# A rewritten first stage with unsplit modulation weights, a new panel order, and eight seven-product gate panels

## The chip, the cores and the metric

The kernel runs on one core of one Trainium2 chip. The metric is the device time of one execution in microseconds (us). Engines: PE (TensorE, matrix products; its weight loads are listed apart as PEld), DVE (VectorE), ACT (ScalarE), POOL (GpSimd), and SP, whose queue issues most transfers.

## The reference

One layer of a decoder trunk runs for a prompt group (1024 tokens) and a sample group (8 sequences of 8 tokens), 1088 tokens in all, with shared weights. The model width is 1024.

- `mod = silu(c) @ w_mod + b_mod` gives shift, scale and gate (each 1024 wide) for nine condition vectors: one of the prompt, eight of the samples.
- `h = rmsnorm(x, norm_g) * (1 + scale) + shift`, and `proj = h @ w_in`, whose columns are three merge gates (mg, 3 x 1024), u, va, za (spatial gating), q, k, v, ob, zb (mLSTM with four heads), p, zc (causal pooling) and eight gate columns.
- Three branches turn these into ya, yb and yc; each is projected (`w_br_a`, `w_br_b`, `w_br_c`), weighted by `sigmoid(mg)`, summed, projected by `w_out`, multiplied by `gate`, added to x and normalised.
- The states of the mLSTM and of the pooling, and the normalised va rows of the samples, are returned too.

All in float32. The kernel keeps the accuracy by splitting a float32 operand into a rounded high part and a low rest (`split`, line 206: a cast on ACT, a subtraction on DVE) and adding three products: high x high, high x low, low x high.

## The kernel before

All instructions of an engine run in the order in which the program issues them; waits between engines are semaphores. Large tiles come from one pool of 34 `slots` (128 x 1088 float32); PSUM has eight banks.

**Weights.** `Stream` (line 37) loads weight panels (1024 x 256) in quarters over SP's queue, and `step` (line 103) splits one quarter: cast on ACT (line 132), subtraction on DVE (line 101). `prep_some` and `seven` call it between matmuls.

**Panels.** `b_panel` (line 258) makes transposed output: six units (two halves of 128 columns by three token groups of 364, 362, 362), each with 8 x 3 matmuls; with `kouter` all six units are open at once and are evicted at the end. `a_panel` (line 296) makes token-major output, nine units of 24 matmuls with 256 columns (16 for the sample unit). `seven` (line 334) makes a panel with seven block products in place of eight: 7 x 2 x 4 x 3 matmuls of 272 columns, the sums of blocks being made on DVE.

**Side work.** Generators in `self.side` are advanced by `tick` between half units; `self.pace` says how many steps a unit gives. Their matmuls stand in PE's list among those of the panels. `drain` runs what is left.

**Order.** `start` (line 466); panels q2 and q3; 25 seven-product panels (k, zb, zc, u, za and five of the twelve mg panels, `MG7 = 5`); p0, va0, p1, va1, ... ; v0 to v3; ob0 to ob3; mg panels 5 to 11; the branch projections in the order c, a, b (four panels each, `finish`, line 1718); the output projection. Gates, spatial gating (`gen_sgu`), gate row (`gen_gate`, line 867), samples (`gen_sample`) and prompt mLSTM (`gen_prompt`) are side work from v0 on.

**The first stage.** A string of letters, `PLAN_0 + PLAN_1` (line 1853), is run letter by letter, and each calls a small function. `1` loads a panel of `w_mod`, `2` an x tile (128 features x 1088 tokens), `3` a weight quarter. `S` splits half a modulation panel, `M` multiplies it (line 548), `C` and `T` copy and turn the result into columns `am` (scale) or `sm` (shift). `Q` squares an x tile on ACT and adds it up on POOL (line 581). `A` or `V` scale x by `am`, `H` and `L` split it. `W` splits a weight quarter; `P` and `R` multiply one x tile with panel q0, later q1: 12 and 6 matmuls (line 614). `e` sums the squares over features with ones as the second operand (line 625), `f` spreads the norm over partitions (line 641). `v` (DVE) or `g` (POOL, line 648) multiply x by the norm, `m` adds the shift and splits the result into the tiles `h` (lines 653 to 660). `z`, `s`, `t` multiply the shift columns with q0 and q1; `r` evicts raw rows. The rows of q0 and q1 get the norm on POOL (line 705) and the shift in `finish_rows`. `gen_factors` (line 757) adds high and low parts again and forms the block sums for `seven`; `put_t4` overwrites part of h with the last of them, after its last use in q3.

Of the kernel before, what the change touches and what calls it, by code (L numbers as in the profile page):

```python
# [32 lines left out]
MG7 = 5  # L33
PACE = 1.5
# [124 lines left out]
class Builder:  # L159
# [98 lines left out]
    def b_panel(self, panel, acts, evac, nk=KT, kouter=False, hook=None):  # L258
# [3 lines left out]
        units = [(f, g) for f in range(2) for g in range(3)]  # L262
# [22 lines left out]
        for u, (f, g) in enumerate(units):  # L285
# [7 lines left out]
            self.tick(self.pace / 2)  # L293
        self.st.used(panel)
# [119 lines left out]
    def body(self):  # L414
# [7 lines left out]
        for nm_, ns in [(x, (n,)) for n in range(4) for x in ("p", "va")] + [(x, range(4)) for x in ("v", "ob")]:  # L422
# [43 lines left out]
    def start(self):  # L466
# [10 lines left out]
        raws, wsp, pmod, xs, xsp = {}, {}, {}, {}, {}  # L477
        panels = (4, 5, 6, 7, 0, 1, 2, 3)

        def mod_load():  # L480
            n = nxt("ml")
            raws[n] = [self.slot([128, 4, 256], name="ss") for _ in range(2)]
            m = 4 if n else 2
            for j in range(0, KT, m):
                S.dma_start(raws[n][j // 4][:, j % 4 : j % 4 + m], i["w_mod"][panels[n]][:, j : j + m, :])
# [6 lines left out]
        cT = self.slot([128, KT, 9], name="cT")  # L492
        S.dma_start(cT, i["cT"])
        mod_load()
        sel = self.cload("sel")
# [17 lines left out]
        self.scs = self.slot([128, KT, 64], F32R, name="scs")  # L513
        V.tensor_copy(self.scs, zero.unsqueeze(1).to_broadcast([128, KT, 64]))
        sc = self.const([128, KT, 9], "sc")
# [3 lines left out]
        A.copy(self.scs[:, :, 0:9], sc)  # L519
        V.tensor_tensor(out=self.scs[:, :, 32:41], in0=sc, in1=self.scs[:, :, 0:9].bitcast(F32), op=ALU.subtract)  # L520
# [9 lines left out]
        def mod_split():  # L530
            n, j = divmod(nxt("ms"), 2)
            raw = raws[n][j]
            hi = self.slot([128, 4, 256], F32R, name="ssh")
            lo = self.slot([128, 4, 256], F32R, name="ssl")
            m = 4 if n else 2
            for q in range(0, 4, m):
                self.split(*(x[:, q : q + m] for x in (raw, hi, lo)))
            wsp.setdefault(n, []).append((hi, lo))
            if j:
                raws.pop(n)  # L540

        def mod_mul():
            n = nxt("mm")
            p = pmod[n] = self.ps()
            w = wsp.pop(n)
            for kk in range(KT):
                for j in range(2):
# [195 lines left out]
        def hook(k):  # L743
            for j in range(2):
                if k == j + 1:
                    self.put_t4(j)
# [1218 lines left out]
```

## Time and profile before

| | us |
|---|---|
| median of 3 runs (1856.19 to 1857.31) | 1856.73 |
| the profiled execution | 1857.86 |
| its span, first to last instruction | 1856.1 |
| busy: PE, DVE, ACT, POOL | 1796.1, 1071.9, 586.0, 262.3 |
| first stage, to the first matmul of q2 | 119.3 |
| to the first matmul of the seven-product panels | 176.9 |
| end of the seven-product panels | 707.3 |

The granted clock of PE has a mean of 0.985; in the profile's strip of 40 slices it is below full in three of the first four slices. A matmul's entry lists the moving operand first, then the stationary one with its rows and columns (`128*128`), then the moving shape. A float32 matmul whose operands aren't split shows as two records.

### The profile page before, as it was taken

To read this page: it belongs to the slowest core of one execution; us is meant where nothing else is said; L and a number is where in the kernel's file an instruction comes from. 1 tells how busy PE (TensorE), PEld (TensorE's weight loads), DVE (VectorE), ACT (ScalarE), POOL (GpSimd) and SP (SyncE) were. 2 spreads that over 40 slices of the span, in tenths; PEclk is the share of its full clock that TensorE was granted. 3 is DMA by queue.
4 is the path that set the end of the run, shared out by engine and by line. 5 is a ranking of instruction groups with operands and counts; after the bars stand their busy time and mean duration, and the time that the engine had idled before them with its cause. 6 is when DMAs were issued, how large, how long until landed. Compare 5 with 4: busy or idle time off the path is not lost.

```text
span 1856.1 us, 32242 instructions
## 1 busy us (share of the span) xinstructions
PE 1796.1 (97%) x13017; PEld 1777.4 (96%) x13017; DVE 1071.9 (58%) x2003; ACT 586.0 (32%) x1141; POOL 262.3 (14%) x427
## 2 busy tenths in 40 slices
PE   7888999999999999999999999999999999999998
PEld 7888999999999998999999899999999999999998
DVE  7777556665666542434527955664655766564444
ACT  5443333333333332222223125332333231131224
POOL 3440000000000001110011212321101101200023
PEclk8988999999999999999999999999999999999999
DMA  6332323332222334333335754776457577694422
GB/s 252 108 128 74 106 94 94 104 122 80 71 70 76 130 106 150 121 123 101 94 116 189 217 180 125 240 237 201 143 175 231 179 228 208 184 317 142 151 62 97
DMA packets 142152, 270.42 MB, mean 146 GB/s; under 512 B 19377, under 2 KB 66161, under 8 KB 142003
## 3 DMA queue, kind: packets, MB, share of 16 engines
q1 hardware_dynamic: 118786, 184.20, 31.4%
q0 software_dynamic: 23072, 83.91, 13.3%
q8 instruction: 102, 1.67, 0.4%
q14 instruction: 48, 0.39, 0.1%
q10 hardware_dynamic: 144, 0.26, 0.0%
HBM read 179.96 MB, written 88.35 MB: 145 GB/s over the span
## 4 chain that ended last, share of the span: by engine, by line
PE 86%; DVE 8%; issue 2%; DMA 2%; ACT 1%; POOL 1%; SPq 0%; POOLq 0%; DVEq 0%; ACTq 0%
PE ps L270 30%; PE ps L308 15%; PE p L362 8%; PE y L362 8%; PE z L362 8%; PE x L362 4%; PE ps L614 2%; PE ps L316 1%; PE ps L1466 1%; PE ps L1264 1%; PE ps L1485 1%; PE ps L1682 1%; PE ps L1439 1%; PE ps L1468 1%; DMA ss<-in_w_mod_dram 1%
## 5 line engine op out<-in xcount | busy, mean ns | idle before, releaser
L101 DVE TENSOR_TENSOR wlo<-raw,whi 128x512 fp32r<-128x512 f32 (+1 forms) x272 | 189.7, 698 | 115.6 <-ACT whi L132 115.6
L308 PE MATMUL ps<-whi,hhi 128*128 128x256 f32 (+1 forms) x768 | 218.5, 284 | 0.0
L308 PE MATMUL ps<-wlo,hhi 128*128 128x256 f32 (+1 forms) x768 | 216.0, 281 | 0.0
L308 PE MATMUL ps<-whi,hlo 128*128 128x256 f32 (+1 forms) x768 | 215.1, 280 | 0.0
L270 PE MATMUL ps<-hhi,whi 128*128 128x362 f32 (+1 forms) x624 | 208.2, 334 | 5.5 <-DVE C L1494 3.4
L270 PE MATMUL ps<-hlo,whi 128*128 128x362 f32 (+1 forms) x624 | 207.0, 332 | 1.9 <-DMA hlo<-b12d 1.7
L270 PE MATMUL ps<-hhi,wlo 128*128 128x362 f32 (+1 forms) x624 | 206.6, 331 | 0.0
L270 PE MATMUL ps<-yhi,whi 128*128 128x362 f32 (+1 forms) x576 | 190.1, 330 | 3.0 <-DVE mgr L1742 1.6
L270 PE MATMUL ps<-yhi,wlo 128*128 128x362 f32 (+1 forms) x576 | 188.7, 328 | 0.0
L270 PE MATMUL ps<-ylo,whi 128*128 128x362 f32 (+1 forms) x576 | 188.5, 327 | 0.0
L132 ACT CAST whi<-raw 128x512 fp32r<-128x512 f32 (+1 forms) x272 | 162.3, 617 | 44.9 <-DVE raw L123 36.3
L308 PEld LDWEIGHTS ps<-whi,hhi 128*128 128x128 f32 x768 | 144.6, 188 | 0.8 <-issue 0.4
L308 PEld LDWEIGHTS ps<-wlo,hhi 128*128 128x128 f32 x768 | 144.7, 188 | 0.0
L308 PEld LDWEIGHTS ps<-whi,hlo 128*128 128x128 f32 x768 | 144.4, 188 | 0.0
L270 PEld LDWEIGHTS ps<-hhi,whi 128*128 128x128 f32 x624 | 119.2, 191 | 6.7 <-DVE C L1494 3.6
L362 PE MATMUL p<-hhi,whi 128*128 128x272 f32 x400 | 116.1, 290 | 7.3 <-ACT row L859 7.3
L270 PEld LDWEIGHTS ps<-hlo,whi 128*128 128x128 f32 x624 | 119.5, 191 | 2.6 <-DMA hlo<-b12d 2.6
L270 PEld LDWEIGHTS ps<-hhi,wlo 128*128 128x128 f32 x624 | 119.4, 191 | 0.0
L362 PE MATMUL p<-hlo,whi 128*128 128x272 f32 x400 | 116.5, 291 | 0.0
L362 PE MATMUL p<-hhi,wlo 128*128 128x272 f32 x400 | 116.3, 291 | 0.0
L132 ACT CAST whi<-sum 128x512 fp32r<-128x512 f32 x75 | 46.6, 621 | 219.7 <-DVE sum L119 144.0
L270 PEld LDWEIGHTS ps<-yhi,whi 128*128 128x128 f32 x576 | 108.2, 188 | 3.7 <-DVE mgr L1742 1.8
(434 smaller groups left out, 4489.6 us busy)
## 6 DMA issues: line engine op xcount, KB each, us to landing
raw<-in_w_in_dram SPq DMA_DIRECT2D x204, 256.0 KB
mgr<-mgd SPq DMA_DIRECT2D x24, 544.0 KB
raw<-in_w_br_dram SPq DMA_DIRECT2D x48, 256.0 KB
out_dram<-C POOLq DMA_DIRECT2D x36, 256.0 KB, 4.5
ylo<-yd SPq DMA_DIRECT2D x16, 544.0 KB
merd<-mgr POOLq DMA_DIRECT2D x16, 544.0 KB, 6.1
C<-in_state_C_dram SPq DMA_DIRECT2D x32, 256.0 KB
mgd<-mg POOLq DMA_DIRECT2D x14, 544.0 KB, 4.6
```

Source lines behind the costliest of these rows:

```text
L101: self.kb.V.tensor_tensor(out=lo, in0=src, in1=hi.bitcast(F32), op=ALU.subtract)
L132: kb.A.copy(hi, src)
L270: self.PE.matmul(ps[:, :n], part(panel, w, k, fs), a[:, g0 : g0 + n], start=(k == 0 and j == 0), stop=(k == nk - 1 and j == 2))
L308: self.PE.matmul(p[:, :cols], a[:, ts], part(panel, w, k, cs), start=(k == 0 and j == 0), stop=(k == KT - 1 and j == 2))
L316: self.PE.matmul(p[:, :cols], stack[:, k, :], part(panel, j, k, cs), start=(k == 0 and j == 0), stop=(k == KT - 1 and j == 1))
L362: PE.matmul(bank[n][:, g, :HT], w[:, ks], b[:, gs], start=(n in (1, 5, 6, 7) and j == 0 and m == 0), stop=(j == 3 and m == 2), skip_group_ ...
L614: PE.matmul(sums[-1][u][:, :m], self.st.part(w, 1 - ww, k, fs), a[:, g0 : g0 + m], start=(k == 0 and part == "high" and j == 0), stop=(k = ...
L1264: self.PE.matmul(p[:, :n], wsl[:, ww, k, fs], a[:, g0 : g0 + n], start=(k == 0 and j == 0), stop=(k == 1 and j == 2))
L1439: PE.matmul(x["ps"][:, h * 128 : h * 128 + 128], k[:, 2 * h + d, :], q[:, 2 * h + d, :], start=(d == 0), stop=(d == 1))
L1466: PE.matmul(p[:, :258], x["qw"][:, 2 * h + d, :], C[x["hp"]][:, h, d, :], start=(d == 0), stop=False)
L1468: PE.matmul(p[:, :258], x["P"][:, a, h, :], x["vs"][:, b, h, :], start=(x["c"] == 0 and j == 0), stop=(j == 2))
L1485: PE.matmul(p[:, :258], x["ks"][:, a, h, d * 128 : d * 128 + 128], x["vs"][:, b, h, :], start=(j == 0), stop=(j == 2))
```

## The change

- **Modulation.** `S`, `C`, `T` are gone. `mod` multiplies the unsplit float32 weights, 128 x 128 at a time as the stationary operand, by the nine columns `sc`, and its result is already turned. The same holds for `gen_gate`, whose result is turned back by eight transposes.
- **Squares.** Each squared tile is summed over its features on PE at once (`square_sum`, letter `U`, nine matmuls with one column) into one bank, in place of the additions on POOL.
- **x and h.** `H` scales and casts in one ACT instruction and `L` scales and subtracts in one DVE instruction, so x stays unscaled; `v` scales by `am` and the norm in one; `m` adds the shift to x in place and splits it. x is kept in float32, and `gen_factors` takes it from there. No tile-wide work is left on POOL in this stage.
- **Plans.** New strings for `PLAN_0` and `PLAN_1`; loads stand two groups ahead.
- **q2, q3.** All four `gen_factors` are side work from q2 on; q3 runs unit by unit with token groups in the order 2, 1, 0, and `put_t4` follows units four and five. `b_panel` gets `order` and calls `hook` after each unit.
- **Order.** p0, v0, p1, v1, ...; then va0 to va3, ob0 to ob3. Side work: gates, samples, spatial gating, sample output (`gen_sample_out`, split off), prompt. `gen_gate` moves under the last branch projection. `MG7` is 8, `PACE` 1.4 throughout.

```diff
-MG7 = 5
-PACE = 1.5
+MG7 = 8
+PACE = 1.4
...
+        units = [divmod(u, 3) for u in order]
...
+            if hook is not None:
+                hook(u)
...
-        for nm_, ns in [(x, (n,)) for n in range(4) for x in ("p", "va")] + [(x, range(4)) for x in ("v", "ob")]:
+        for nm_, ns in [(x, (n,)) for n in range(4) for x in ("p", "v")] + [(x, range(4)) for x in ("va", "ob")]:
...
+        def mod():
+
             n = nxt("mm")
...
+            raw = raws.pop(n)
             p = self.ps()
...
             for j in range(2):
...
+                v = p[:, j * 16 : j * 16 + 9]
+                for kk in range(KT):
+                    PE.matmul(v, raw[kk // 4][:, kk % 4, j * 128 : j * 128 + 128], sc[:, kk, :], start=(kk == 0),
+                              stop=(kk == KT - 1))
...
+        def square_sum():
+            k = nxt("us")
+            sq = sqs.pop(k)
             if k == 0:
...
+                acc.append(self.ps())
+            for t in range(9):
+                m = 128 if t < 8 else 64
+                PE.matmul(acc[0][:m, t : t + 1], sq[:, t * 128 : t * 128 + m], ones, start=(k == 0 and t == 0),
+                          stop=(k == KT - 1), skip_group_check=True)
...
+        def h_scale():
+            k = nxt("hs")
+            x = xs[k]
+            V.scalar_tensor_tensor(out=x[:, :TP], in0=x[:, :TP], scalar=am[:, k, 0:1], in1=rb[0][:, :TP], op0=ALU.mult,
+                                   op1=ALU.mult)
+            V.tensor_tensor(out=x[:, smp], in0=x[:, smp], in1=rb[0][:, smp], op=ALU.mult)
+            V.tensor_tensor(out=bview(x[:, smp]), in0=bview(x[:, smp]), in1=bcol(sm[:, k, 1:9]), op=ALU.add)
...
+            A.activation(x[:, :TP], x[:, :TP], AF.Identity, bias=sm[:, k, 0:1])
+            self.split(x, hh, hl)
...
+        while len(self.side) > 2:
+            self.advance(self.side)
+
+        def hook(u):
+            if u == 2:
+                self.drain()
+            if u > 3:
+                for j in range(2):
+                    self.put_t4(2 * u - 8 + j)
+
+        self.b_panel(self.pan["q", 3], self.h, self.evac_rows(3, self.qd), hook=hook, order=(2, 1, 0, 5, 4, 3))
...
+                for k in range(KT):
+                    PE.matmul(p[:, j * 16 : j * 16 + 9], w[k // 4][:, k % 4, j * 128 : j * 128 + 128], self.sc[:, k, :],
+                              start=(k == 0), stop=(k == KT - 1))
...
+        self.side += [self.gen_gates(), self.gen_sample(), self.gen_sgu(), self.gen_sample_out(), self.gen_prompt()]
...
+                if n == 0 and xi == 2:
+                    self.side.append(self.gen_gate())
...
 Builder.PLAN_0 = (
-    "wSS3w21M2W2CT1QVwSH4SL2wPQMV2Q1CWTHR21VSPHLSPMQ3Q2RVHLRLCTPVWSRHL23SPWQQMC3RVTHAHLLwPRQV3H"
-    "LPSSRPR1WS3"
+    "1223w 1223QQwMHHWLLw 1223UUQQMPHHWPLLRR 1223UUQQMPHHWPLLRR 13UUQQMPHHWPLLRR 13UUWPPRRe"
 )
 Builder.PLAN_1 = (
-    "rW13SeSM1CPP3MS3PCfRTSgMCgPWSvRgTMgCRTvRTPzmWRmsmgPmPWmWgPRRmtms3R3WmW3tr"
+    "r13WMfPR fW13MPRvm PRvmWPRvmM 33PRvm33PRvmMzs PRvmWWPRvmsWW vmr"
 )
```

More of the change, by code (lines that the diff above doesn't have):

```diff
@@ L482, in mod_load @@
             raws[n] = [self.slot([128, 4, 256], name="ss") for _ in range(2)]
-            m = 4 if n else 2
-            for j in range(0, KT, m):
-                S.dma_start(raws[n][j // 4][:, j % 4 : j % 4 + m], i["w_mod"][panels[n]][:, j : j + m, :])
+            for j in range(2):
+                S.dma_start(raws[n][j], i["w_mod"][panels[n]][:, 4 * j : 4 * j + 4, :])
         def x_load():
@@ L528, in start @@
         self.h = []
[L530 to L542, printed above, removed]
-            n = nxt("mm")
[L544 to L547, printed above, removed]
-                    PE.matmul(p[:64, :256], self.scs[:, kk, :], w[kk // 4][j][:, kk % 4, :],
-                              start=(kk == 0 and j == 0), stop=(kk == KT - 1 and j == 1))
-        def mod_copy():
-            n = nxt("mc")
-            t = self.tmp.tile([64, PW], F32, tag="smp", name=self.nm("smp"), bufs=2)
-            A.copy(t[:, :256], pmod[n][:64, :256])
-            pmod[n] = t
-        def mod_turn():
-            n = nxt("mt")
-            t = pmod.pop(n)
+        def mod():
+            n = nxt("mm")
+            raw = raws.pop(n)
             p = self.ps()
-            if n == 0:
-                V.tensor_scalar(bmod[:, 1, :], bmod[:, 1, :], 1.0, None, ALU.add)
             for j in range(2):
-                PE.matmul(p[:, j * 16 : j * 16 + 9], t[:, j * 128 : j * 128 + 128], sel, start=True, stop=True)
+                v = p[:, j * 16 : j * 16 + 9]
+                for kk in range(KT):
+                    PE.matmul(v, raw[kk // 4][:, kk % 4, j * 128 : j * 128 + 128], sc[:, kk, :], start=(kk == 0),
+                              stop=(kk == KT - 1))
             for j in range(2):
@@ L617, in mms, with rms @@
                 xsp[k] = None
-            if n == KT - 1 and part == "low":
-                self.st.units -= 4
-        def rms_sum():
-            p = self.ps()
-            for t in range(9):
-                m = 128 if t < 8 else 64
-                PE.matmul(p[:m, t : t + 1], acc[0][:, t * 128 : t * 128 + m], ones, start=True, stop=True)
+        def rms():
+            p = acc.pop()
             ms = self.const([128, 9], "ms")
@@ L631, in rms_sum @@
             self.rsqrt(rs, ms, rt)
[L632 removed]
+            rb.append(self.slot([128, T], name="rb"))
         def rms_rows():
[L635 to L644 removed]
@@ L646, in h_scale @@
-        def h_scale(eng):
-            x = xs[nxt("hs")]
-            eng.tensor_tensor(out=x, in0=x, in1=rb[0], op=ALU.mult)
+            b = nxt("rr")
+            t0, t1 = ((0, 4), (4, 9))[b]
+            ps = [self.ps() for _ in range(-(-(t1 - t0) // 4))]
+            for t in range(t0, t1):
+                m = 128 if t < 8 else 64
+                o = (t - t0) % 4 * 128
+                PE.matmul(ps[(t - t0) // 4][:, o : o + m], rs[:m, t : t + 1].to_broadcast([m, 128]), self.ident[:m, :m],
+                          start=True, stop=True)
```

212 lines of the change are left out of this document (84 added, 128 removed).

## The prediction

> **What bounds the kernel now.** I read the page first, then busy time by stage, then the chain of waits and the order of PE's work in the first 180 us.
>
> ```profile
> span 1856.1 us, 32242 instructions
> PE 1796.1 (97%) x13017; PEld 1777.4 (96%) x13017; DVE 1071.9 (58%) x2003; ACT 586.0 (32%) x1141; POOL 262.3 (14%) x427
> ```
>
> PE is the bound: what lengthens its list lengthens the kernel, unless it lands in idle time of PE. Nearly all of that lies early, as the table by stage shows (columns: stretch, its length, busy time of PE, PEld, DVE, ACT and POOL with instructions, granted clock, DMA share, GB/s):
>
> ```profile
> 0.00:119.30 119.30, 95.05 (x604) 89.30 (x604) 92.28 (x108) 57.36 (x81) 49.87 (x31) 0.89 0.47 166
> 119.30:143.00 23.70, 23.70 (x130) 23.69 (x130) 14.62 (x23) 11.81 (x20) 7.79 (x7) 0.89 0.50 173
> 143.00:176.80 33.80, 26.59 (x161) 26.30 (x159) 30.01 (x37) 12.96 (x23) 1.06 (x2) 0.93 0.08 26
> 176.80:707.30 530.50, 530.43 (x4200) 530.22 (x4200) 305.46 (x461) 179.64 (x303) 21.81 (x42) 0.99 0.30 96
> ```
>
> The rows are the first stage, panel q2, panel q3 and the 25 seven-product panels. Only the first and third have slack. The chain says why:
>
> ```profile
> 106.25 7.89 DVE x L653
> 119.38 22.41 PE ps L270 x120
> 174.64 2.18 ACT row L859 x6
> 176.87 5.78 PE p L362 x24
> 182.64 3.02 PE y L362 x24
> 1201.36 3.99 PE ps L270 x24
> ```
>
> ```profile
> 116.00 0.21 DVE L653 TENSOR_TENSOR x<-x,sm 128x64 f32<-128x64 f32 x1
> 109.13 4.92 POOL L705 TENSOR_TENSOR row<-row,rb 128x1088 f32<-128x1088 f32 x2
> ```
>
> An addition over 64 columns that elsewhere takes 0.21 us held VectorE for 7.9 us while POOL multiplied rows of the same stage (the change moves that work off POOL); q3 with its six banks open ended in six evictions, with PE idle for 7.3 us; and the first seven product then took 5.78 us against 3.02 for a later one.
>
> **Part 1, dense prices.** Full-clock matmuls cost 3.99/24 = 0.166 us in a b-panel and 3.02/24 = 0.126 in a seven-product panel. A b-panel has 144 (23.9 us), a seven panel 168 (21.2). Three panels changed: 3 x 2.7 = **-8.1 us**. Their VectorE work lies under PE: 305 us busy of 530 in that stage, 12 a panel; without that cover it would cost up to 3 x 12 us.
>
> **Part 2, tiny matmuls.** The new `mod` multiplies 128x128 weights by nine columns: 16 matmuls a panel; `square_sum` has nine with one column for each x tile. The nearest rows:
>
> ```profile
> 60.16 2.04 PE L625 MATMUL ps<-ones,acc 128*128 128x1 f32 x18
> 71.79 2.31 PE L641 MATMUL ps<-c_ident,rs 128*128 128x128 f32 x18
> 37.19 1.02 PE L564 MATMUL ps<-c_sel,smp 64*128 64x9 f32 x4
> 48.10 0.61 PE L564 MATMUL ps<-c_sel,smp 64*128 64x9 f32 x4
> 8.87 0.28 PE L548 MATMUL ps<-ssl,scs 128*64 128x256 f32 x1
> 28.58 0.28 PE L548 MATMUL ps<-ssh,scs 128*64 128x256 f32 x1
> 28.70 0.28 PE L548 MATMUL ps<-ssl,scs 128*64 128x256 f32 x1
> L897 PE MATMUL ps<-wgs,scs 128*64 128x256 f32 x64 | 7.9, 276 | 0.0
> ```
>
> Nine matmuls are 18 records at 0.112 us, so two a matmul. `mod` is then 32 x 0.112 = 3.6 us and one x tile's sum 2.0. Removed are 16 x 0.115 (starts 28.58 to 28.70) = 1.8 and a turn of 0.6. Over eight of each, PE's list grows by 8 x 1.2 + 7 x 2.0 = 24 us, more than the 119.3 - 95.1 = 24 us that PE idles. `gen_gate`, now under the last branch, goes from 64 x 0.115 = 7.4 us to 128 x 0.112 plus eight transposes at 0.11 = 15.2: **+7.8 us**, since PE is dense there.
>
> [...]
>
> **Part 3, the clock, which decides.** At 37.19 the same four records cost 1.02 us, not 0.61: the clock was at half. It changes in steps of 3.41 us. Stretches cut at those steps (PEclk is the third number from the end):
>
> ```profile
> 86.90:90.31 3.41, 1.90 (x12) 1.65 (x12) 2.71 (x6) 0.00 (x0) 0.04 (x1) 1.00 0.00 0
> 90.31:93.72 3.41, 3.41 (x13) 3.38 (x14) 1.96 (x7) 1.93 (x5) 0.17 (x1) 0.50 0.00 0
> 711.54:714.95 3.41, 1.94 (x12) 1.56 (x10) 0.00 (x0) 0.24 (x1) 0.47 (x2) 1.00 1.03 418
> 714.95:718.36 3.41, 1.75 (x7) 0.75 (x5) 0.00 (x0) 0.49 (x2) 0.30 (x2) 1.00 1.03 397
> 1080.18:1083.59 3.41, 2.04 (x17) 1.81 (x16) 3.38 (x6) 0.38 (x1) 0.58 (x1) 1.00 0.64 243
> 1083.59:1087.00 3.41, 3.41 (x17) 3.18 (x16) 1.15 (x1) 0.00 (x0) 1.67 (x2) 0.50 0.73 163
> 1493.19:1496.60 3.41, 1.85 (x13) 1.64 (x12) 2.03 (x5) 0.00 (x0) 0.00 (x0) 1.00 0.73 224
> 1496.60:1500.01 3.41, 3.41 (x26) 3.41 (x25) 3.24 (x14) 0.47 (x1) 1.51 (x2) 1.00 0.05 11
> ```
>
> Busy time doesn't order them: after 1.90 and 2.04 us the clock fell, after 1.94 and 1.85 it stayed. What does is that the first two held narrow matmuls:
>
> ```profile
> 88.41 0.61 PE L564 MATMUL ps<-c_sel,smp 64*128 64x9 f32 x4 [1.78 <-DVE sm L571]
> 88.95 1.26 PE L614 MATMUL ps<-xlo,whi 128*128 128x364 f32 x6
> 1082.38 1.07 PE L1029 MATMUL ps<-c_w_sguS,va 64*128 64x64 f32 x8 [1.36 <-ACT tok L971]
> 40.72 0.50 PE L614 MATMUL ps<-xhi,whi 128*128 128x362 f32 x1
> 41.02 0.51 PE L614 MATMUL ps<-xhi,wlo 128*128 128x362 f32 x1
> ```
>
> Between 86.90 and 90.31 only six wide matmuls (6 x 0.166 = 1.0 us, 29%) count, if nine-column ones do not. I take it that streamed columns keep the clock up and records do not. In the new stage `UUM` is 68 tiny records, 7.6 us without a wide matmul, over two steps long, ahead of `PPRR`, 36 wide ones in 6.0 us. At half clock a wide one costs 0.30 (40.72 to 41.02) and, in that ratio, a tiny one 0.2; the clock returns after one wholly wide step, as at 1083.59.
>
> **Part 4, the first stage summed.** From when the first weights are in (about 7 us; the old first panel's last product starts at 8.87): `M U U M` is 100 records, the clock falls near 8.4: 12 x 0.112 + 88 x 0.2 = 19, to 26. `PPRR` then has half clock until one whole step has passed, on average 1.5 steps = 5.1 us (17 matmuls), the other 19 at 0.166: 8.3, to 34.3. Two further groups: on average 5.1 us at full clock (46 records), 22 x 0.2 = 4.4, then 8.3: 17.8 each, to 69.9. `UU PPRR`: 4.0 + 8.3, to 82. The second part is four `M` (14.3), eight `PR` (8 x 18 x 0.166 = 23.9), the broadcasts of the norm (2.3, as at 71.79) and two shift products (2 x 1.84): 44; a lone `M` of 3.6 us, scarcely one step, loses about 2, so +8: PE reaches q2 at 134.
>
> Beside it runs a chain on VectorE and ScalarE, in which `v m` works one x tile at a time, each step waiting for the other engine:
>
> ```profile
> L658 DVE SCALAR_TENSOR_TENSOR hlo<-x,sm,hhi 128x1024 fp32r<-128x1024 f32 x8 | 10.2, 1278 | 4.4 <-ACT hhi L656 4.3
> L656 ACT ACTIVATE hhi<-x,sm 128x1024 fp32r<-128x1024 f32 x8 | 9.2, 1147 | 0.0
> L595 ACT CAST xhi<-x 128x1088 fp32r<-128x1088 f32 x8 | 8.8, 1098 | 12.8 <-DVE x L590 12.8
> L208 DVE TENSOR_TENSOR t<-fac,t 128x1088 fp32r<-128x1088 f32 x4 | 5.1, 1284 | 1.1 <-ACT t L207 1.1
> ```
>
> 1.28 + 1.15 + 1.10 + 1.28 and hops make 5.0 us a tile, 40 for eight, 44 with five weight splits and the shift. It starts when the norm's rows are out (82 + 12 = 94) and ends at 138, when q2's first unit asks for the last tile (134 + 3.5). I add 4 us for what meets there: a bank for the sixth `M`; the shift product, which waits for its split with the last two `PR` queued behind it on PE; the last tile, for which the whole of q2 waits. Bounds: 0 and twice that. What gets late next is q2, which ends at 138 + 4 + 20.5 = 162.5. The turn of the shift (0.9), q3 now unit by unit (23.9) and one eviction (0.7) bring the first seven product to **188**, against 176.87: +11.1. Its product then runs at full clock: 3.02 - 5.78 = -2.8. At nothing I cost `gen_factors` and `finish_rows` (about 32 us of VectorE under q2 and q3, 48 us) and the new order of v, va and the samples, whose matmuls and loads are the same. The first stage's loads come in groups on SP's queue, two groups ahead of PE, with nothing else on it; the gate's eight loads now stand on that queue among those of the last branch. The bounds for these are in the rivals.
>
> Sum against the profiled execution's 1857.9: +11.1 - 2.8 - 8.1 + 7.8 = +8.0, so 1865.9; the median shown is 1.1 below it: **1865 us**.
>
> **The rivals.** *The clock holds (faster).* If weight loads count as activity, PE has no idle step and all is at 0.112 and 0.166: `PPRR` of the first group ends at 7 + 11.2 + 6 = 24.2, two groups of 13.6 and one of 10 bring 61.4, the norm's rows are out at 71, the chain ends at 115, q2 at 135.5, and with 3 us for the idle PE before it the seven products start at 164: -12.9 - 2.8 - 0.3 = -16, **1841**. For it: no narrow stretch of over 2.3 us is in the trace. Against it: with narrow ones counted in full, 1.90 us should have held the clock as 1.85 and 1.94 did. It decides if the granted clock is 1.00 through a `UUM`.
>
> [...]
>
> *Only the long stretches fall.* A lone `M` costs nothing and the chain of 44 sets q2: the four us added and 2 of the chain's start go, 182: **1859**.
>
> *A late stall (slower).* The samples now run before the gating unit, whose two constant tiles are then still held, among 34 slots. If each of their 32 steps waits 0.3 us for a load, 10 us come on top: **1875**. The same price covers a merge load that waits behind the gate's on SP. Against it, the longest wait of these products in the old run:
>
> ```profile
> PE ps L1682 <- DVE Cs L208: 0.5, 1, 0.5
> ```
>
> *The seven panels give nothing*, if VectorE can't keep up: +8.1, **1873**; 58% busy there speaks against it.
>
> **How the numbers follow.** Forecast 0.47, only long stretches 0.12, late stall 0.08, seven panels nothing 0.04, clock holds 0.29. The range is 1839 to 1876; the likeliest's own is 1858 to 1873. A measurement of this kernel can tell about 0.2%, 3.7 us: faster 0.29, same 0.13 (the second rival and the forecast's lower end), slower 0.58.
>
> **What will show it.** Granted clock near 0.5 to 0.8 in slices one to three with PE busy throughout; tiny records at 0.2 us; the first seven product near 188 us and at 3.0; the gate's records at 0.112 under the last branch. The forecast is wrong if the clock stays at 1.00 there, or if q2 starts before 125 us.

## The result and the profile after

The changed kernel takes **1898.25 us** (median of 4 runs, 1895.33 to 1901.06) against 1857.02 for the kernel before (4 runs, 1856.19 to 1858.02): a ratio of 1.0222, 95% interval 1.0204 to 1.0239. It is 41 us slower, 33 us over the forecast of 1865 and outside its range. The profiled execution took 1898.14 us.

The head of the page of the changed kernel, busy time and the 40 slices:

```profile
span 1896.0 us, 32907 instructions
PE 1847.7 (97%) x13367; PEld 1830.7 (97%) x13367; DVE 1033.1 (54%) x2016; ACT 585.5 (31%) x1123; POOL 213.3 (11%) x410
...
POOL 0000000000000000010101223322101101200023
PEclk6789999999999999999999999999999999999999
```

PE is as busy as before (97%), with 350 instructions more. What stands out is the granted clock, well below full in the first three slices, 142 us. The same by stage (columns: stretch, its length, busy time of PE, PEld, DVE, ACT and POOL with instructions, granted clock, DMA share, GB/s); the first row is the kernel before up to its first seven product, the others are the changed kernel:

```profile
0.00:176.90 176.90, 145.37 (x893) 139.32 (x893) 136.92 (x167) 82.15 (x122) 58.73 (x40) 0.90 0.40 140
```

```profile
0.00:198.30 198.30, 192.37 (x1099) 190.10 (x1099) 82.34 (x149) 68.97 (x98) 10.57 (x23) 0.79 0.36 129
...
198.00:789.00 591.00, 590.74 (x4703) 590.74 (x4704) 338.69 (x511) 202.61 (x341) 25.57 (x48) 1.00 0.30 96
789.00:1896.00 1107.00, 1064.61 (x7568) 1049.89 (x7567) 612.08 (x1357) 314.20 (x686) 177.14 (x339) 0.98 0.52 170
```

Three differences make up the 40.3 us between the two profiled executions:

- **First stage: +21.4 us.** The first seven product starts at 198.3 instead of 176.9. PE now idles only 6 us there (198.3 - 192.4) where it idled 31.5, but its clock averages 0.79 instead of 0.90. Length times clock is 159 us of full-clock time before and 157 after, which suggests, without showing it, that with the clock of before the stage would be no longer than it was.
- **Seven panels: as forecast.** 28 in 591.1 us, 21.1 each; 25 took 530.4.
- **Late part: 21.7 us over the forecast's account.** From the last seven product (789.4) to the end it is 1106.6 us, against 1148.8 from 707.3 on before. Three panels of 23.9 us less and 7.8 of gate more would have given 1084.9. (21.4 + 60.7 - 42.2 = 39.9, the difference of the spans.)

The waits of TensorE behind the first stage (columns: the matmul that waited and for whom; total us, times, longest):

```profile
PE ps L1637 <- DVE qz L1601: 13.3, 3, 6.8
PE ps L986 <- DVE va L976: 8.0, 5, 4.0
PE ps L270 <- DMA hlo<-b12d: 2.6, 2, 1.7
PE ps L1637 <- ACT Cs L207: 2.3, 2, 1.3
PE ps L1637 <- DVE Cs L208: 2.3, 4, 1.2
```

L1637 is the sample product, L1682 in the kernel before, where it waited 0.7 us in all. Now it waits 17.9, most of it at three points, where the samples pass from one head to the next (L1601). Summed over the gaps between all matmuls behind the last seven product, PE idles 32.4 us against 18.6 before. The rest of the 21.7, some 8 us, is records that take longer: 36.7 us of this part go by at half clock, against 14.7 before. The falls stand at 797.8 (10.2 us, where the first panel behind the sevens waits for its transfers `hlo<-b12d`; 3.4 us at the same place before), at the two longest waits of the samples (6.8 us at 1122.1, 10.2 at 1180.1) and at the longest of the gating unit (L986, 3.4 us at 1221.0); the rest is at the very end. The matmuls behind the first of the samples' two cost 0.21 us each, where 12 of them in a dense panel take 1.38 us, 0.115 each:

```profile
1122.98 1.20 PE L1637 MATMUL ps<-Cs,qz 128*128 128x258 f32 x4 [4.93 <-DVE qz L1601]
...
1124.62 0.42 PE L310 MATMUL ps<-wlo,hhi 128*128 128x256 f32 x1
1124.83 0.42 PE L310 MATMUL ps<-whi,hlo 128*128 128x256 f32 x1
```

### The profile page after: what moved, and what is told of

The parts are those of the page before. It is cut to its first block, busy times and chain, and to the rows that moved or that the text cites. A ratio compares the mean times of both kernels' runs of the same rounds, so it can differ in the third digit from the quotient of the medians.

```text
span 1896.0 us, 32907 instructions
## 1 busy us (share of the span) xinstructions
PE 1847.7 (97%) x13367; PEld 1830.7 (97%) x13367; DVE 1033.1 (54%) x2016; ACT 585.5 (31%) x1123; POOL 213.3 (11%) x410
## 5 line engine op out<-in xcount | busy, mean ns | idle before, releaser
L270 PE MATMUL ps<-yhi,whi 128*128 128x362 f32 (+1 forms) x576 | 190.9, 331 | 0.6 <-DVE vo L1463 0.6
L270 PE MATMUL ps<-yhi,wlo 128*128 128x362 f32 (+1 forms) x576 | 188.6, 327 | 0.0
L270 PE MATMUL ps<-ylo,whi 128*128 128x362 f32 (+1 forms) x576 | 188.4, 327 | 0.0
L270 PE MATMUL ps<-hhi,whi 128*128 128x362 f32 (+1 forms) x480 | 161.2, 336 | 3.5 <-ACT hhi L207 1.8
L270 PE MATMUL ps<-hlo,whi 128*128 128x362 f32 (+1 forms) x480 | 160.6, 335 | 3.6 <-DMA hlo<-b12d 2.6
L270 PE MATMUL ps<-hhi,wlo 128*128 128x362 f32 (+1 forms) x480 | 159.8, 333 | 0.0
L364 PE MATMUL p<-hhi,whi 128*128 128x272 f32 x448 | 128.7, 287 | 0.6 <-ACT row L824 0.6
L364 PE MATMUL p<-hlo,whi 128*128 128x272 f32 x448 | 129.1, 288 | 0.0
L364 PE MATMUL p<-hhi,wlo 128*128 128x272 f32 x448 | 128.9, 288 | 0.0
L132 ACT CAST whi<-sum 128x512 fp32r<-128x512 f32 x84 | 52.1, 620 | 245.5 <-DVE sum L119 165.6
L270 PEld LDWEIGHTS ps<-yhi,whi 128*128 128x128 f32 x576 | 108.4, 188 | 0.9 <-DVE vo L1463 0.9
L270 PEld LDWEIGHTS ps<-ylo,whi 128*128 128x128 f32 x576 | 108.4, 188 | 0.1
L270 PEld LDWEIGHTS ps<-yhi,wlo 128*128 128x128 f32 x576 | 108.4, 188 | 0.0
L270 PEld LDWEIGHTS ps<-hlo,whi 128*128 128x128 f32 x480 | 92.4, 192 | 5.2 <-DMA hlo<-b12d 4.0
```

The source lines that it names most:

```text
L132: kb.A.copy(hi, src)
L270: self.PE.matmul(ps[:, :n], part(panel, w, k, fs), a[:, g0 : g0 + n], start=(k == 0 and j == 0), stop=(k == nk - 1 and j == 2))
L364: PE.matmul(bank[n][:, g, :HT], w[:, ks], b[:, gs], start=(n in (1, 5, 6, 7) and j == 0 and m == 0), stop=(j == 3 and m == 2), skip_group_ ...
```

## The experiments

Two questions: is it the clock that makes the first stage long, and what makes the samples wait? My theory for the first is the forecast's part 3 (narrow matmuls do not hold the clock); the rival is that the narrow records cost what they cost. For the second I began with late state loads, against a burst of VectorE work, the new order, and lack of room beside the shorter late part.

| kernel | what differs | us, median | ratio to before, 95% |
|---|---|---|---|
| changed | | 1898.3 | 1.0204 to 1.0239 |
| e_mix | narrow and wide matmuls 1 : 1 | 1925.0 | 1.0326 to 1.0385 |
| e_fill | a zero matmul behind each narrow one | 1981.0 | 1.0647 to 1.0680 |
| e_rows | modulation streams the weights | 1903.6 | 1.0236 to 1.0285 |
| e_pool | and squares summed on GpSimd | 1883.3 | 1.0123 to 1.0171 |
| e_chain | and first stage reordered | 1877.8 | 1.0106 to 1.0139 |
| e_order | later panels in the old order | 1900.4 | 1.0216 to 1.0251 |
| e_order5 | and five mg panels as sevens | 1887.6 | 1.0149 to 1.0179 |
| e_load | state loads one pair earlier | 1893.5 | 1.0172 to 1.0216 |
| e_head | masked keys made step by step | 1918.5 | 1.0315 to 1.0345 |
| e_slots | two constant tiles loaded late | 1883.3 | 1.0128 to 1.0162 |
| e_slotload | e_slots and e_load | 1877.3 | 1.0101 to 1.0131 |
| e_best2 | e_chain and e_slotload | 1858.0 | 0.9996 to 1.0032 |
| e_best3 | and two waits removed | 1863.9 | 1.0022 to 1.0050 |
| e_best4 | and the gate from split weights | 1850.7 | 0.9957 to 0.9978 |

### The clock: e_mix and e_fill

In `e_mix` each narrow matmul becomes an entry of a queue that is emptied by one behind each wide matmul (the letters of the plan are put in an order that fits, and the first modulation panel, which has no wide ones beside it, gets zero matmuls of 128 columns):

```diff
+        def pop(n=1):
+            while narrow and n:
+                narrow.pop(0)()
+                n -= 1
...
+                for kk in range(KT):
+                    narrow.append(lambda j=j, kk=kk: mm(j, kk))
...
                               start=(k == 0 and part == "high" and j == 0), stop=(k == KT - 1 and part == "low"))
+                    pop()
```

> The changed kernel with one thing altered: the narrow fp32 matmuls of the first stage (modulation, L535, and sums of squares, L557) are issued one after each wide matmul of q0 and q1 (L588) instead of in stretches of their own; the first modulation panel, which has no wide matmuls beside it, gets a 128-column zero matmul after each of its own. No product is taken away; about 24 zero matmuls are added. Theory (the clock: TensorE is granted half clock because the narrow stretches stream too few columns): the granted clock stays at 1.00 through the first stage, a narrow record takes 0.11 us instead of 0.22, q0 and q1 end near 68 us instead of 87.7, the first seven product starts at 175 to 181 us instead of 198.3, and the time falls by 17 to 22 us to about 1879. Rival (a narrow fp32 record simply costs 0.22 us there, whatever stands beside it, or the modulation weights arrive too late): the first stage is as long as before this edit or longer by the zero matmuls, 1896 to 1903 us.

It took 27 us more than the changed kernel. The stages of `e_mix`:

```profile
25.00:39.00 14.00, 14.00 (x104) 13.61 (x105) 4.36 (x11) 6.31 (x9) 0.00 (x0) 0.98 0.53 209
39.00:107.00 68.00, 68.00 (x274) 66.02 (x274) 9.56 (x25) 7.98 (x12) 1.81 (x1) 0.50 0.15 50
107.00:143.00 36.00, 36.00 (x263) 35.61 (x262) 14.50 (x27) 12.96 (x17) 3.51 (x6) 1.00 0.34 115
```

For 14 us the clock held, then, from near 38.5, it was half for 68 us in which PE was busy every moment. So neither expectation came true: the narrow records are not dear in themselves (they were cheap for 14 us), but mixing didn't keep the clock. Rows from both stretches, the same pair of one wide and one narrow matmul:

```profile
36.00 0.42 PE L615 MATMUL ps<-xlo,whi 128*128 128x362 f32 x1
36.26 0.28 PE L581 MATMUL ps<-ones,sq 128*128 128x1 f32 x2
36.40 0.41 PE L615 MATMUL ps<-xlo,whi 128*128 128x362 f32 x1
...
60.45 0.65 PE L615 MATMUL ps<-xlo,whi 128*128 128x362 f32 x1
60.90 0.42 PE L581 MATMUL ps<-ones,sq 128*128 128x1 f32 x2
61.17 0.65 PE L615 MATMUL ps<-xlo,whi 128*128 128x364 f32 x1
```

A pair takes 0.40 us at full clock and 0.72 at half. At 0.166 for the wide one, the pair streams at most 0.166 / 0.40 = 42% of its time. That lies on the edge here, as the steps of 3.41 us show in which the clock changes (the wide matmuls alone; `x` counts those that run into the step too):

```profile
24.86:28.27 3.41, 3.35 (x9) 1.72 (x9) 1.00 1.01 405
35.10:38.51 3.41, 3.27 (x9) 1.53 (x8) 1.00 0.00 0
38.51:41.93 3.42, 3.18 (x6) 1.81 (x6) 0.50 0.00 0
103.36:106.78 3.42, 3.19 (x10) 2.80 (x11) 0.50 0.38 125
106.78:110.19 3.41, 3.41 (x16) 2.38 (x14) 1.00 0.07 29
```

At full clock 9, 9, 8 and 8 wide matmuls start in the four steps; behind the first three the clock held, behind the fourth it fell. At half clock the same mixture, a pair in 0.72 us, has only 4 to 6 of them in a step, and the clock stayed at half for 68 us. It came back behind the first step with nine, where the narrow ones had run out. In the changed kernel every group ends in 36 wide matmuls in a row, and the clock came back within them, at 29.8, 50.3, 70.8 and 84.4 us. Half the theory stood and the remedy was wrong.

About 20 such steps with PE busy throughout (68.00 us of the 68 from 39 to 107) went by at half clock in `e_mix`, so busy time alone did not bring the clock back here.

`e_fill` keeps the order and adds work: a matmul of zeros, 128 columns wide, behind each of 136 narrow ones.

```diff
+                    if n < 4:
+                        PE.matmul(p[:64, 64:192], zero, zwide, start=False, stop=False, skip_group_check=True)
...
+                PE.matmul(acc[0][:64, 64:192], zero, zwide, start=False, stop=False, skip_group_check=True)
```

> The changed kernel in its own order, with work added: after every narrow matmul of the first four modulation panels and of the sums of squares (64 + 72 = 136 of them) one 128-column matmul of zeros into unused columns of the same PSUM bank, about 0.22 us each at full clock, 30 us of added TensorE work in all; nothing is computed differently. Theory (the clock): the granted clock stays at 1.00 through the first stage, a narrow record takes 0.11 us, and the 30 us added are about paid by the 25 to 30 us that the stretches lose now, so the time stays within 8 us of 1898. Rival (the narrow records cost what they cost): the whole 30 us appear, 1925 to 1932 us. If the clock fell anyway the added matmuls would take 0.44 us each and the time would be over 1950.

The third branch came, 1981 us: the clock fell at 11.7 and PE then ran at half:

```profile
12.00:62.00 50.00, 50.00 (x184) 36.21 (x184) 4.95 (x13) 6.79 (x10) 0.00 (x0) 0.50 0.41 163
```

The filler was thinner than I took it to be: a narrow and a zero matmul together cost 0.68 us at full clock, not 0.44. By my estimate from the slope between a matmul of 272 columns (0.126 us) and one of 362 (0.166), 128 columns stream for about 0.06 us; counted once for each of its two records, that is under a fifth of the time. In this run the clock was 0.50 from 12 to 62 us with it. That the filler's data are zeros is not the reason by itself: in `e_mix` a step at half clock that held nothing but the same filler, 17 records in 3.83 us, was followed by full clock at 24.9:

```profile
21.16 3.83 PE L508 MATMUL ps<-zwide,zero 128*64 128x128 f32 x17
```

### The clock: e_rows, e_pool and e_chain

`e_rows` turns the modulation product round, so that weights are streamed, and puts one narrow sum of squares behind each of those and behind every second wide matmul:

```diff
-                    PE.matmul(v, raw[kk // 4][:, kk % 4, j * 128 : j * 128 + 128], sc[:, kk, :], start=(kk == 0),
-                              stop=(kk == KT - 1))
+                PE.matmul(p[:9, :256], sc[:, kk, :], raw[kk // 4][:, kk % 4, :], start=(kk == 0), stop=(kk == KT - 1))
+                pop()
...
+            A.copy(t[:9, :256], p[:9, :256])
...
+                PE.matmul(p[:, j * 16 : j * 16 + 9], t[:9, j * 128 : j * 128 + 128], self.sel[:9, :], start=True, stop=True)
```

> The changed kernel with the modulation product of each panel turned round: the 9 columns of conditioning are the stationary side and the unsplit weights, 256 columns wide, are streamed (8 matmuls instead of 16, two records of about 0.22 us each instead of 0.11, so 3.5 us at full clock instead of 3.6), then one copy and two small matmuls turn the result back. The sums of squares stay narrow, but one is issued behind each wide modulation matmul and behind every second matmul of q0 and q1, never in a stretch of their own. Theory (the clock falls in a step in which less than about 38% of the time is streamed, and comes back only after a step that is streamed nearly wholly; the kernel with one narrow matmul behind each wide one stood at 37 to 39% and fell into it): every step is now above 45%, the clock stays at 1.00, the first seven product starts at 174 to 182 us instead of 198.3, and the time is 1873 to 1883 us. Rival (the cost of the narrow products is not the clock's): TensorE's work is the same and the first stage as long, 1893 to 1903 us.

1903.6 us, near the rival's number, yet its trace refutes the rival. Its second and third groups are the same list of matmuls (`P M P T R R` with 18 sums of squares between):

```profile
15.60:45.10 29.50, 29.46 (x97) 21.37 (x97) 5.05 (x10) 8.41 (x13) 0.00 (x0) 0.50 0.60 239
45.20:60.60 15.40, 15.34 (x89) 10.97 (x88) 2.55 (x8) 2.63 (x5) 0.00 (x0) 1.00 0.25 84
61.70:78.40 16.70, 16.30 (x92) 11.69 (x92) 4.15 (x9) 4.26 (x7) 0.00 (x0) 1.00 0.25 74
78.40:100.00 21.60, 20.15 (x128) 16.84 (x128) 7.00 (x18) 4.69 (x11) 1.81 (x1) 1.00 0.37 120
```

29.5 us at half clock, 15.4 at full: **the same group took 1.9 times as long at half the granted clock.** The mixture that held the clock here, two wide matmuls and one narrow:

```profile
63.46 0.41 PE L607 MATMUL ps<-xhi,whi 128*128 128x362 f32 x1
63.71 0.33 PE L607 MATMUL ps<-xhi,wlo 128*128 128x362 f32 x1
63.88 0.28 PE L573 MATMUL ps<-ones,sq 128*128 128x1 f32 x2
64.02 0.41 PE L607 MATMUL ps<-xhi,whi 128*128 128x364 f32 x1
```

That is 2 x 0.166 in 0.56 us, 59%, at 1.00 from 45 to 100 us. But the group that came first entered at half clock, behind waits of 1.9 us for the turn of the first modulation and 0.9 for `xhi`, and as in `e_mix` the clock did not rise under the mixture, for 29.5 us: it came back at 45.2, behind the first step with ten wide matmuls. That cost some 14 us, which ate the gain; the later waits for the turned product (4.8 us the longest) did the rest.

`e_pool` is `e_rows` with the squares added on GpSimd as in the kernel before, so that 63 narrow matmuls go.

```diff
+                G.tensor_tensor(out=acc[0], in0=acc[0], in1=sq, op=ALU.add)
...
-                PE.matmul(acc[0][:m, t : t + 1], sq[:, t * 128 : t * 128 + m], ones, start=(k == 0 and t == 0),
-                          stop=(k == KT - 1), skip_group_check=True)
+                    PE.matmul(p[:m, t : t + 1], acc[0][:, t * 128 : t * 128 + m], ones, start=True, stop=True)
```

> The kernel of e_rows with the squares added up on GpSimd, as in the kernel before, so that TensorE issues 9 sums of squares instead of 72. Theory (TensorE's own work sets the end of the first stage once the clock is whole): 63 matmuls of 0.22 us, 14 us, go from the path; the first seven product starts at about 162 us and the time is 1858 to 1866 us. Rival (the loads of x and of the weights, or GpSimd's seven additions of 2.9 us, set the end): no more than 4 us under e_rows.

20 us under `e_rows`. The theory's price for the 63 matmuls is 14 of them; besides, the first stretch at half clock lasts 6.8 us in place of 30.8, so the run does not separate the two. The level was 20 us over what I had worked out, since `e_rows` was. `e_chain` then mends the order of the first stage (a modulation panel ahead of the panels that don't need it, `v` one tile ahead of `m`) and puts the copy of the first four modulation products on VectorE.

```diff
-    "1223w 1223QQwWMwTHHLLw 1223QQPMPTHHWLLRR 1223QQPMPTHHWLLRR 13QQPMPTHHWLLRR 13WPUPRR.e"
+    "1223w 1223QwWMwwTwwHHQLL 1223QQPMPTHHWRRLL 1223QQMPTPHHWRRLL 13QQMPTPHHWRRLL 13WPUPRR.e"
-    "r13WMfPTRf W13MPRTvm PRvm WPRvmM 33TPRvm33PRvmMTzs PRvmWWPRvmsWW vmr"
+    "r13WMfPTRf W13MPRTv PRvm WPRMvm 33TPRvm 33PRMvm TzPRsvm WWPRsvm WWvmmr"
```

> The kernel of e_pool with the order of its first stage mended where its trace shows TensorE waiting: the copy of a modulation product on VectorE for the first four panels, a modulation panel ahead of the q panels whose inputs it does not feed, and in the second part each tile scaled (L621) one tile ahead of the split that ends the tile before it, so that VectorE no longer stands still for 1.96 us in each tile while ScalarE makes hhi. Theory (with the clock whole, the first part is bound by TensorE's 10 us a group and the second by the chain of about 5 us a tile, which becomes 3.6): the first seven product starts at 148 to 158 us instead of 179.3 and the time is 1852 to 1862 us. Rival (the second part is bound by TensorE and the modulation panels, not by the chain): only the first part gains, 1865 to 1875 us.

1877.8, 3 us over the rival's bound. Its stages:

```profile
0.00:17.00 17.00, 12.87 (x111) 10.26 (x112) 3.22 (x10) 5.31 (x7) 0.43 (x7) 0.94 0.78 271
17.00:62.00 45.00, 40.93 (x218) 32.51 (x217) 27.81 (x38) 17.24 (x26) 21.08 (x8) 0.95 0.56 210
62.00:113.00 51.00, 48.89 (x283) 38.21 (x282) 22.61 (x45) 18.37 (x29) 6.30 (x9) 1.00 0.30 101
113.00:170.00 57.00, 53.35 (x294) 50.87 (x292) 41.28 (x62) 28.46 (x42) 3.73 (x7) 0.91 0.31 111
```

The first part ends near 62 us instead of 87.7, at clock 0.95. The second still takes 51 us: PE is busy for 48.9 of them, so it is PE's own list, and not the chain on VectorE, that bounds it once the chain is shortened. The first seven product starts at 170.4, 28 us earlier than in the changed kernel and 6.5 earlier than before the change.

### The late part: e_order, e_order5

`e_order` puts the later panels, their side work and the paces back in the old order, keeping first stage, eight mg panels as sevens and gate.

```diff
-        self.side += [self.gen_gates(), self.gen_sample(), self.gen_sgu(), self.gen_sample_out(), self.gen_prompt()]
+                self.side += [self.gen_gates(), self.gen_sgu(), self.gen_sample(), self.gen_sample_out(), self.gen_prompt()]
...
-            self.a_panel(self.pan["v", g], self.h, self.hs, self.evac_tok(g, self.vd, "copy"), cols=256 if g else 264)
+            self.a_panel(self.pan["va", g], self.h, self.hs, self.evac_tok(g, self.vad, "gelu"))
```

> The changed kernel with the later panels and their side work put back into the order of the kernel before: p and va alternate, then v, then ob; gates, sgu, samples and prompt behind the first v panel; paces 1.2, 1.5 and 1.4. First stage, eight mg panels as seven products and the new gate stay. Theory (the samples, moved under the faster panels of 96 and 108 us, make TensorE wait): the idle time before the sample matmuls of L1637 goes, and the time falls by 15 to 24 us to about 1877. Rival (the late part is longer for another cause, for instance more weight splitting per panel): no change, 1895 to 1902 us.

No gain: the late part is 1106.9 us, as in the changed kernel (1106.6). The samples' waits fell by more than half, but new ones came in the prompt (L1462) and the last branch (`ylo`), where the kernel before and the changed one had little:

```profile
PE ps L1640 <- DVE qz L1604: 6.6, 3, 2.3
PE ps L988 <- DVE va L978: 5.8, 5, 1.5
PE ps L1462 <- DVE vo L1323: 5.1, 1, 5.1
PE ps L270 <- DVE ylo L208: 4.8, 4, 1.8
```

So the old order doesn't fit beside the shorter late part. `e_order5` gives it back its room:

```diff
-MG7 = 8
+MG7 = 5
```

> The kernel of e_order (first stage and gate of the changed kernel, later panels and side work in the order of before) with five instead of eight mg panels as seven products, so three more panels of 23.9 us behind the samples. Theory (cover: the side work of samples, prompt and gate no longer fits beside the shorter late part, and whatever the order it appears as waits and half clock, some 21 us): the waits go back to what they were before the change, and the time is 1882 to 1890 us although the dense matmuls cost 8.1 us more. Rival (the place of the samples or their loads, not the room beside them): the 8.1 us are simply added, 1905 to 1911 us.

1887.6: the theory of cover. Its late part is 1160.2 us, against 1148.8 before the change plus 7.1 for the gate. In the old order the three seven panels gained 8.1 in matmuls and cost 1900.4 - 1887.6 + 8.1 = 21 in cover. No run has the new order with five.

### The late part: e_load, e_head, e_slots, e_slotload

`e_load` asks for the samples' state tiles one pair earlier:

```diff
+        load(2)
-                load(x // 2 + 2)
+                load(x // 2 + 3)
```

> The changed kernel with the state tiles of the samples (L1591) asked for one pair earlier: three pairs are in flight instead of two. Nothing else is altered. Theory (late loads: the DVE work of a head change at L1601 and L1605 stands behind a split that waits for its state tile): the waits of L1637, 17.9 us, and most of the loss from the half clock behind them go, and the time falls by 12 to 22 us to about 1881. Rival (the head change's own 12 VectorE instructions, some 4.5 us in one step, are too much for one step): the waits at the head changes stay within 3 us of what they are, 1893 to 1900 us.

Between the two: 4.8 us less, and the samples' waits are 10.0 instead of 17.9. `e_head` makes the masked keys of the next head step by step, which takes two tile slots more:

```diff
-            for b in range(8):
-                V.tensor_scalar(km[b // 4][:, b % 4, :], kst[b // 4][:, h, :].bitcast(F32), self.bmask[:, b % 4 : b % 4 + 1], None, ALU.mult)
...
+            km_one(h + 1, bb)
```

> The changed kernel with the masked keys of the next head (L1605, eight VectorE instructions of 0.3 us) made one in each sample step instead of eight in the last; loads as they are. Theory (late loads: what stands at the head change is a split that waits for its state tile): the wait of L1637 for qz falls by the burst alone, from 13.3 to about 9 us, and the time by 2 to 6 us, 1892 to 1896. Rival (the burst of VectorE work is the cause): the wait falls under 3 us and the time by 12 to 18 us, 1880 to 1886.

Both expectations failed: 20 us **more**, and the samples wait 29.3 us. Apart from its place in time the VectorE work is the same; what the edit takes besides is two slots. What then is late is seen in ScalarE's waits during the samples (the split of a state tile, L207, waits for GpSimd's last write into that tile, which follows its load). In order: before, changed, `e_head`:

```profile
ACT Cs L207 <- POOL C L1638: 18.1, 8, 3.6
```

```profile
ACT Cs L207 <- POOL C L1593: 43.0, 11, 7.7
```

```profile
ACT Cs L207 <- POOL C L1593: 50.4, 12, 7.8
```

The waits of the state load itself fit. On its queue it waits until a tile is given back, most often until the store of an older state is done:

```profile
SPq L1591 <- DMA out_dram<-C: 26.9, 7, 7.4
```

Such waits of the state loads add up to about 75 us before, 89 in the changed kernel and 110 in `e_head`. This is what the forecast's third rival names: the samples run ahead of the gating unit, whose two constant tiles are still held, among 34 slots. `e_slots` loads and masks these two when the unit starts:

```diff
-        self.w_sguT = self.slot([128, NH, 128], name="sgc")
-        self.bsgu = self.slot([128, 8, 128], name="bsgu")
...
         a, nxt = load(0), load(1)
+        self.w_sguT = self.slot([128, NH, 128], name="sgc")
+        self.bsgu = self.slot([128, 8, 128], name="bsgu")
```

> The changed kernel with the two constant tiles of the spatial gating unit (sgc, bsgu) loaded and masked when that unit starts, behind the samples, instead of ahead of the later panels; before the change the unit ran ahead of the samples and had given them back by then. Nothing else moves. Theory (the samples are short of tile slots: a state load waits for the slot of an older tile, as the 20 us rise showed when two more slots were taken for masked keys): with two slots more the state loads start earlier, the waits of L1637 (17.9 us) fall under 9 us and the time by 9 to 17 us, 1881 to 1889. Rival (the steps come too fast under the faster panels, whatever the slots): no change, 1894 to 1902 us.

1883.3, 15 us less. The state loads wait about 74 us, ScalarE's wait is 27.5 instead of 43.0, TensorE's in the samples 6.0 instead of 17.9, although the gating unit's first tile now waits 8.1:

```profile
ACT Cs L207 <- POOL C L1595: 27.5, 11, 4.1
```

```profile
PE ps L977 <- DVE va L967: 8.1, 1, 8.1
PE ps L1639 <- DVE qz L1603: 4.8, 3, 2.4
PE ps L1639 <- DVE Cs L208: 1.2, 1, 1.2
```

`e_slotload` is `e_slots` with the edit of `e_load`:

> The kernel of e_slots with the state tiles also asked for one pair earlier, as in e_load. Theory (slots and late loads): the waits of L1637 shrink to the VectorE burst of the three head changes, some 6 us, half clock included; 1878 to 1886 us, 8 to 15 us under e_load. Rival (only the request was late, and e_load has already taken all there is): within 3 us of e_load, 1890 to 1897 us.

1877.3, 16 us under `e_load`: the theory. The late part is 1089.6 us, 17 of the 22 us back (the other 4 of the 21 lie in the first stage, which the edit leaves alone: in the seven kernels that share it the first seven product starts between 194.6 and 198.3), and the samples' waits are down to 5.8 us, most of it still at the head changes.

### Both together: e_best2, e_best3, e_best4

> The kernels of e_chain and of e_slotload together. If the two causes are independent, their gains add: 1835 to 1847 us, under the 1857 of the kernel before. Rival (a later wait takes the place of what is saved): 1850 or over.

1858.0, level with the kernel before. That is the rival's number. By the medians the gains add, 1898.3 - 20.5 (`e_chain`) - 20.9 (`e_slotload`) = 1856.9, and I had counted on more from each. By the profiled executions they don't quite: the spans of the two promise 1871.0 + 1875.3 - 1896.0 = 1850.3, and it is 1856.8, with a late part of 1095.2 us against 1089.6 in `e_slotload` and 11.3 us of waits in the gating unit against 8.9. So a part may well have gone to a later wait; the runs of `e_best2` lie between 1851.6 and 1866.5, too far apart to tell. `e_best3` sends the copy of a modulation product back to ScalarE and has the gating unit ask earlier for its first tiles:

```diff
-            (V.tensor_copy if n < 4 else A.copy)(t[:9, :256], p[:9, :256])
+            (A.copy if n else V.tensor_copy)(t[:9, :256], p[:9, :256])
...
         a, nxt = load(0), load(1)
+        lg = self.slot([128, D], name="lng")
...
+        yield
+        yield
```

> The kernel of e_best2 with two waits of its trace removed: the copy of a modulation product goes back to ScalarE except for the first panel (it stood behind the low-part splits on VectorE, 3.8 us of idle TensorE and a step at half clock), and the gating unit asks for its first two tiles ahead of its constants and lets three more side steps pass before it needs them (7.1 us of idle TensorE). Theory (those two waits are what is left): 8 to 13 us under e_best2, 1845 to 1850 us, under the kernel before. Rival (the waits move to the next product): within 4 us of e_best2, 1854 to 1862 us.

The rival: no gain, 1863.9. The gating unit's waits fell to 4.0 us, but later ones rose (5.4 for L270 on `ylo`), and the first seven product didn't move (170.5). `e_best4` computes the gate from split weights, as the kernel before did, at its new place:

```diff
-                    PE.matmul(p[:, j * 16 : j * 16 + 9], w[k // 4][:, k % 4, j * 128 : j * 128 + 128], self.sc[:, k, :],
-                              start=(k == 0), stop=(k == KT - 1))
+                    PE.matmul(p[:64, :256], scs[:, k, :], w[k // 4][j][:, k % 4, :],
+                              start=(k == 0 and j == 1), stop=(k == KT - 1 and j == 2))
```

> The kernel of e_best3 with the gate computed from split weights again (64 matmuls of 256 columns and the splits that go with them, as in the kernel before), at the place where the changed kernel has it, beside the last br panels. Theory (TensorE is the bound there, so the gate costs its records: 13.6 us with 128 small ones, 7.3 us with 64 wide ones): 5 to 8 us under e_best3. Rival (the splits on ScalarE and VectorE, which the unsplit form saves, hold the br panels' own work up): no gain, or a loss of up to 5 us.

1850.7 us, 13 under `e_best3` by the medians and 8.4 by the profiles (late part 1086.8 against 1095.4), and **0.33% under the kernel before** (0.43 to 0.22%). From start to start, less waits, the gate's records and transposes cost 15.9 us in `e_best3` and its 64 records 7.3 here: 8.6 us, about what the profiles differ by. The gate's price is on the path. `e_best4` beats both kernels.

## Why the prediction was wrong

**The direction and two of the four terms held.** Slower was given 0.58. Part 1: a seven panel costs 21.1 us, as forecast. Part 2: the narrow matmuls do come as two records; the gate's 128 and its transposes cost 7.1 us more than the 64 wide ones, forecast 7.8, and `e_best4` shows that this is paid.

**Part 3, what the clock does, held.** In the changed kernel it fell while PE was busy with narrow matmuls, and a narrow record then cost 0.21 us (32 of them take 6.85, from 39.77 to 46.62); 0.2 was assumed. `e_mix` (0.50 for 68 us of busy PE) and `e_rows` (the same group in 29.5 us at 0.50 and in 15.4 at 1.00) bear it out. That streamed columns are what keeps the clock up was my reading: the runs show only how many wide matmuls start in a step. The likeliest rival, that the clock holds, is excluded: it needed 1.00 through a `UUM`. So is the second one, that a lone `M` costs nothing: the clock fell behind each of the four, at 91.2, 101.5, 118.5 and 128.8. A row of the changed kernel's second group, the modulation alone, says what a `UUM` got:

```profile
39.80:46.70 6.90, 6.90 (x34) 6.90 (x33) 0.00 (x0) 0.00 (x0) 0.00 (x0) 0.50 0.06 21
```

**Part 4, the first stage's sum, was mis-sized by 10 us (forecast 188, measured 198.3).** The term that failed first is the group: 17.8 us by "on average 5.1 us at full clock" ahead of each fall, 20.0 measured. The full clock lasts two steps, 6.8 us, in each group, and the wide matmuls use up some 4 of them; 2.3 and 2.8 us are left for the two narrow stretches, as the step in which they begin holds too few wide ones already (six start between 33.2 and 36.6). So some 45 and not 22 of the 68 tiny records cost 0.21 us. That and the last group put the end of q0 at 87.7 instead of 82. Second, the chain on VectorE was to start at 94 and started at 102.7: 5.7 us from the groups, and 3 because its first scaling stands on VectorE behind the columns of the second modulation panel in this part (L543), which PE gives out only at 102.4. Third, the chain took 47.1 us instead of 44 (one 4.8 us wait for `hhi`). The rest came 1.5 us shorter than forecast: 8.7 + 3.1 - 1.5 = 10.3.

```profile
DVE hlo L208 <- ACT hhi L207: 18.4, 8, 4.8
...
DVE sm L543 <- PE ps L535: 5.6, 3, 2.9
```

**The costing at nothing of the new order failed, by 22 us.** "The new order of v, va and the samples, whose matmuls and loads are the same" left out who holds the slots. The late-stall rival named exactly this, but was given 0.08 and 10 us: 0.3 us for each of 32 steps. The waits in fact are 17.9 us, 13.3 of them at three head changes, and the two longest bring 6.8 and 10.2 us at half clock on top. `e_slots` and `e_slotload` give back 15 to 21 us of the total, 17 of it within the late part; of the remaining 5 us, the trace of `e_slotload` has 2.8 us more of idle PE between matmuls than the kernel before (22.3 against 19.5) and 6.8 us more at half clock, 3.4 of them right behind the seven panels. What makes these longer wasn't tested.

The range, which ended at 1876, failed on the late part: its 22 us alone take 1865 to 1887. The late stall and a longer first stage were besides treated as alternatives. They are independent, and both came: 1865 + 10 + 22 = 1897.

## What to carry to other kernels

Read the granted clock next to the busy time: a stage at 97% busy (192.4 of 198.3 us) lost a fifth of its speed to half clock (0.79). Here narrow matmuls did better in one block between long wide ones (changed, 1898.3 us), or turned so that the wide operand streams (`e_rows`, 1903.6), than in an even mixture (`e_mix`, 1925.0): at half clock 4 to 6 wide matmuls of it started in a step, against 8 or 9 at full clock, and it stayed there for 68 us. Before side work is moved past other side work, list the buffers each holds while the other runs; two tile slots held too long cost 15 us here.

## What the runs showed of the hardware

- **The clock followed the wide matmuls of a step.** The traces give the granted clock in stretches at 1.00 or 0.50, each but the last a whole number of steps of 3.41 us (18 stretches in the kernel before, 28 in the changed one). A mixture with 42% wide time lost the clock (`e_mix`), the group with the 59% mixture held it (`e_rows`), and once at half clock both stayed there, for 68 and nearly 30 us. That looks like two limits; counted in wide matmuls they are one here. I divided all 16 traces into these steps and counted the wide matmuls (362 or 364 columns) that start in each, leaving out steps with others of more than 9 columns. Behind ten or more the next step ran at full clock, in 1861 of 1861 steps at full clock and 95 of 95 at half (120 of 120 and 4 of 4 in the kernel before, 115 of 115 and 7 of 7 in the changed one); behind seven or fewer it ran at half, in 104 of 104 and 136 of 136 (6 of 6 and 6 of 6 before, 10 of 10 and 14 of 14 changed). Only eight or nine went both ways. At 0.166 us each, eight to ten are 39 to 49% of a step at full clock; at half clock, at 0.30 each, they are 70 to 88% of it, so that such a step had to be nearly full of wide matmuls. This is a count over these traces; what lies behind it they do not show.
- **A small wait cost twice.** In the changed kernel a wait of 4.9 us at 1118 was followed by a granted clock of 0.50 from 1122.1 to 1128.9, and by matmuls at 0.21 us instead of 0.115.
- **Mixing hid little.** At full clock a wide and a narrow matmul in turn took 0.40 us (`e_mix`, at 36.00), what they take one after the other (0.166 + 2 x 0.112 = 0.39).
